# A tensor-bound backbone step: weights and moving columns placed at a fixed distance modulo 256 bytes

## The chip, the cores and the metric

The kernel runs on one core of one Trainium2 chip. The metric is the device time of one execution in microseconds (us), lower is better. The times are medians of several runs; beside them stands one execution under the hardware profiler, with its own time.

## The reference

One inference step of a two-layer backbone over 640 tokens (512 latent, 128 context) with 1024 channels. Layer 0 mixes tokens with a bidirectional state-space scan (SSD), layer 1 with differential attention. After each mixer comes a gated channel mixer with a convolution of width 3 between its two matrix products. Cut to what matters here:

```python
for i in range(DEPTH):                       # DEPTH = 2
    hp, hs = modulate(xp, ...), modulate(xs, ...)
    # mixer: i == 0: SSD; i == 1: differential attention
    op, os_ = mixer(hp), mixer(hs)
    xp = xp + p_g1 * op;  xs = xs + s_g1 * os_
    xp = xp + p_g2 * conv_ffn(modulate(xp, ...), *ffn_p)
    xs = xs + s_g2 * conv_ffn(modulate(xs, ...), *ffn_p)

def conv_ffn(h, up_w, conv_w, conv_b, down_w):
    u = dwconv(h @ up_w, conv_w, conv_b)     # 1024 -> 5632 channels
    a, v = jnp.split(u, 2, axis=-1)
    return (jax.nn.silu(a) * v) @ down_w     # 2816 -> 1024 channels
```

Everything is float32, and the products with weights are by far the most work.

## The kernel before

Activations lie channel-major: 128 channels on the partitions, the 640 tokens in a row of 2560 bytes in each partition. A float32 product is made of three fast ones: each operand is split into a high and a low part of type float32r, and the kernel adds high·high, high·low and low·high. These are called the dense products below.

A dense product is a chain of matmul instructions that add into one output. Each matmul holds a block of 128 x 128 weights in the array (the stationary operand; the profile shows its load as PEld) and streams 256, 320 or 384 columns of an activation tile past it (the moving operand). `dense_many` runs over the 8 (or 4, or 6) blocks of channels, over the three pairs high·high, high·low, low·high, and over the two halves of the tokens, "A" with 256 columns and "B" with 384, so that matmuls of 256 and 384 columns alternate and each pair of them works off 640 columns. Where one half alone is run (in `start_tiles` and at the end of `project_last`), many matmuls of one width follow each other. In the feed-forward layers, from the sixth block of channels on, `pair8` and `begin7` use a scheme with seven products instead of eight for blocks of 2 x 2 (tiles `T1` to `T3` hold sums of activations, tiles `s` sums of weights); all its matmuls have 320 columns.

While one matmul runs, the weights of the next one are loaded. So two streams read the on-chip memory at once: the moving columns of the running matmul, and the weight columns of the next one.

Tiles come from pools. `self.pw` ("wts") holds raw weights and their parts `whi` and `wlo`, three buffers each; `self.ph` ("acts") holds activations, among them the split activations with the tags `hh` and `hl` (printed as `h00h`, `h01l` and so on); in each feed-forward layer a pool of its own holds the split products `mh` and `ml`, which are the moving operand of the second matrix product, and two more buffers each for weight parts (`xhi`, `xlo`; they print as `whi` and `wlo` as well). `cast` makes the parts and chooses the pool: with a feed-forward pool open, two of every five weight units go to its `x` buffers, or a unit's own entry says so. A pool takes its address from what lies ahead of it, and a tile its address from the order in which its tag is first used. Each of these tiles, and each slice of one that a matmul takes, is a multiple of 256 bytes long in a partition, so a tag has one address modulo 256 in all of its buffers and slices.

Nearly all instructions stand under line 95 of the code, since a helper issues them; the tiles tell them apart: `po` is an output projection (from `mh`, `ml` in the feed-forward layers), `up` the first product of a feed-forward layer, `x`, `z`, `bc` the products into the scan, `q`, `k`, `v` those of the attention, `st` the first tiles after a normalization.

Of the kernel before, what the change touches and what calls it, by code (L numbers as in the profile page):

```python
# [11 lines left out]
F32 = mybir.dt.float32  # L12
# [8 lines left out]
P = 128  # L21
# [43 lines left out]
class Op:  # L65

    def __init__(self, engine, call, args, kw, dur, occ):
        self.engine, self.call, self.args, self.kw = engine, call, args, kw
        self.dur, self.occ = dur, occ
        self.real, self.end = None, 0.0  # L70
# [285 lines left out]
class Step:  # L356


    def __init__(self, ctx, tc, a):
        self.ctx, self.tc, self.nc, self.a = ctx, tc, Engines(self, tc.nc), a  # L360
        self.later = None
        self.tasks = []
        self.ticks = 0
        self.wi = 0
        self.normt = {}
        self.ready = []
        self.px = None
        self.modtask = None
        self.late = []
        self.wraw, self.wcast = {}, {}  # L370
        self.s, self.summed = {}, set()
        self.deep = 1
        self.units = []
        pool = lambda n, b, **k: ctx.enter_context(tc.tile_pool(name=n, bufs=b, **k, reuse_waits="tile"))
        self.pc = pool("const", 1)
        self.pw = pool("wts", 2)
        self.ph = pool("acts", 1)
        self.xctx = ExitStack()
        self.xd = None
        self.psb = None  # L380
        self.psm = pool("psm", 1, space=PSUM)
        self.dram = pool("dram", 1, space=bass.MemoryType.DRAM)
# [100 lines left out]
    def cast(self, upto):  # L483
        while len(self.wcast) <= min(upto, len(self.units) - 1):
            u = len(self.wcast)
            self.prefetch(u)
            n = self.units[u][1]
            r = self.wraw[u]
            kind = self.units[u][2]
            place = self.units[u][3] or ("x" if self.px and u % 5 > 2 else "w")  # L490
            wp, t, b = (self.pw, "w", 3) if place == "w" else (self.px, "x", 2)
            hi = wp.tile([P, 1024], F32R, tag=t + "hi", name=f"whi{u}", bufs=b)
            lo = wp.tile([P, 1024], F32R, tag=t + "lo", name=f"wlo{u}", bufs=b) if u else None
            if u == 0:
                half = lambda t, j: t.rearrange("p (k j m) -> p k j m", k=KT, j=2)[:, :, j, :]
                r3 = r[:, :n].rearrange("p (k m) -> p k m", k=KT)
                self.act(half(hi, 0), r3, AF.Copy)
                self.tt(half(hi, 1), r3, half(hi, 0).bitcast(F32), ALU.subtract)
            elif isinstance(kind, tuple):
                ns, j0, ia, iv = kind  # L500
                self.prefetch(u + iv)
                ra, rv = self.wraw[u + ia], self.wraw[u + iv]
                w = ns * P
                for j in range(j0, j0 + 1024 // w):
                    x = self.slot("f", f"s{j}", bufs=NF)[:, :w]
                    a, b, op = ((rv[:, :w], rv[:, w:2 * w], ALU.add), (self.s.get(0), ra[:, :w], ALU.subtract),
                                (ra[:, :w], rv[:, :w], ALU.subtract), (ra[:, w:2 * w], self.s.get(1), ALU.subtract))[j]
                    self.tt(x, a, b, op)
                    self.s[j] = x
                    c = slice(w * (j - j0), w * (j - j0 + 1))  # L510
                    self.act(hi[:, c], x, AF.Copy)
                    self.tt(lo[:, c], x, hi[:, c].bitcast(F32), ALU.subtract)
            else:
                c = slice(kind or 0, n)
                if u in self.summed:
                    with self.urgent(1.2):
                        self.act(hi[:, c], r[:, c], AF.Copy)
                        self.act(lo[:, c], r[:, c], AF.Copy, scale=-1.0)
                        self.nc.gpsimd.dma_start(lo[:, c], self.units[u][0][:, c], accum_op=ALU.add)
                else:  # L520
                    self.act(hi[:, c], r[:, c], AF.Copy)
                    self.tt(lo[:, c], r[:, c], hi[:, c].bitcast(F32), ALU.subtract)
            self.wcast[u] = (hi, lo)

    def nextw(self):
        u = self.wi
        self.wi += 1
        self.prefetch(u + 2 + self.deep)
        self.cast(u + self.deep)
        return self.wcast[u]  # L530
# [499 lines left out]
    def ffn(self, l, h, nextnorm, pool):  # L1030
# [17 lines left out]
        def epilogue(p, ua, uv):  # L1048
            ca = self.tmp("ca")
            self.conv(ca, ua, cw[:, p, :])  # L1050
            cv = self.tmp("cv")
            self.conv(cv, uv, cw[:, FT + p, :])
            self.act(ca, ca, AF.Silu)
            self.tt(cv, ca, cv, ALU.mult)
            hi = self.slot("mh", f"mh{p}", F32R, bufs=MIDS, pool=pool)
            lo = self.slot("ml", f"ml{p}", F32R, bufs=MIDS, pool=pool)
            self.act(hi, cv, AF.Copy)
            if p + 1 not in ends:
                self.act(lo, cv, AF.Copy, scale=-1.0)
                nc.gpsimd.dma_start(lo, cv, accum_op=ALU.add)  # L1060
            else:
                self.tt(lo, cv, hi.bitcast(F32), ALU.subtract)
            mid[p] = (hi, lo)
# [66 lines left out]
        def pair8(p, more):  # L1130
# [27 lines left out]
            with self.tc.high_priority():  # L1158
                self.act(uv[:, lft], X, AF.Copy)
            epilogue(p, ua, uv)  # L1160

        def finish_operands():
# [744 lines left out]
    def run(self):  # L1907
        tc, nc, a = self.tc, self.nc, self.a
        self.units = self.weight_units()
        name = lambda u: self.units[u][0] is not None and self.units[u][0].name  # L1910
        up = [u for u in range(len(self.units)) if name(u) == a["w_up"].name]
        after = {u for u in up if name(u - 1) and name(u - 1) != a["w_up"].name}
        after |= {u + 3 for u in after if name(u + 1) is False}
        half = len(up) // 2
        self.summed = (set(up) - set(up[:5]) - set(up[half:half + 5]) - after)
        qkv = [u for u in range(len(self.units)) if name(u) == a["w_qkv"].name]
        self.summed |= set(qkv[8:])
        self.x = []

        def norm(l, s, h):  # L1920
            def mk(hf):
                if hf == "A":
                    h.extend(self.new_h(f"h{l}{s}"))
                return self.norm_task(hf, self.gs[l][s], self.shift(l, s), h)
            return mk

        hs = [[] for _ in range(4)]
        psd = lambda: tc.tile_pool(name="psd", bufs=3, space=PSUM, reuse_waits="tile")
        psb = lambda: tc.tile_pool(name="psb", bufs=6, space=PSUM, reuse_waits="tile")
        self.open_x()  # L1930
        scond = ExitStack()
        sp = scond.enter_context(tc.tile_pool(name="scond", bufs=1, reuse_waits="tile"))
        with psd() as self.psd:
            with tc.tile_pool(name="first", bufs=1, reuse_waits="tile") as pool, tc.manual_schedule():
                self.silu_cond(sp)
                dtps = self.first_tiles(hs[0], pool)
            with (tc.tile_pool(name="sconst", bufs=1, reuse_waits="tile") as cp,
                  tc.tile_pool(name="ssd", bufs=1, reuse_waits="tile") as pool):
                self.ssd_consts(cp)
                self.ssd(hs[0], dtps, norm(0, 1, hs[1]), pool)  # L1940
        scond.close()
        with psb() as self.psb, tc.tile_pool(name="ffn0", bufs=1, reuse_waits="tile") as pool:
            self.px = pool
            self.late = [lambda: self.slot("f", "ntl", bufs=NF)] * 3
            self.ffn(0, hs[1], norm(1, 0, hs[2]), pool)
            self.px = None
        self.psb = None
        self.deep = 1
        with psd() as self.psd:
            self.attention(hs[2], norm(1, 1, hs[3]))  # L1950
        with psb() as self.psb, tc.tile_pool(name="ffn1", bufs=1, reuse_waits="tile") as pool:
            self.px = pool
            self.ffn(1, hs[3], self.final_task, pool)
            for t in reversed(list(self.tasks)):
                self.drain(t)
        self.xctx.close()
# [99 lines left out]
```

## Time and profile before

| | us |
|---|---|
| median of 3 runs (1797.16 to 1798.43) | 1798.12 |
| the profiled execution's own time | 1797.76 |
| its span, first to last instruction | 1796.0 |
| mean granted clock of TensorE | 0.996 |

The span falls into these stretches: up to 40 us the start; to 421 us the scan; to 548 us its output projection; to 1000 us the first feed-forward layer; to 1256 us the attention; to 1340 us its output projection; to 1796 us the second feed-forward layer. A matmul's duration in the profile is modelled and holds its passage through the array: matmuls that follow each other overlap in it. So their speed is not read from the mean duration but from the distance between their starts, here called the step.

### The profile page before, as it was taken

To read this page: it belongs to the slowest core of one execution; us is meant where nothing else is said; L and a number is where in the kernel's file an instruction comes from. 1 tells how busy PE (TensorE), PEld (TensorE's weight loads), DVE (VectorE), ACT (ScalarE), POOL (GpSimd) and SP (SyncE) were. 2 spreads that over 40 slices of the span, in tenths; PEclk is the share of its full clock that TensorE was granted. 3 is DMA by queue.
4 is the path that set the end of the run, shared out by engine and by line. 5 is a ranking of instruction groups with operands and counts; after the bars stand their busy time and mean duration, and the time that the engine had idled before them with its cause. 6 is when DMAs were issued, how large, how long until landed. Compare 5 with 4: busy or idle time off the path is not lost.

```text
span 1796.0 us, 33598 instructions
## 1 busy us (share of the span) xinstructions
PE 1763.9 (98%) x12786; PEld 1687.8 (94%) x12786; DVE 1473.8 (82%) x2947; ACT 1172.3 (65%) x2313; POOL 150.2 (8%) x180
## 2 busy tenths in 40 slices
PE   7999999999999999999999999999999999999997
PEld 5899899989989999999999999999889999999997
DVE  5789999999966869788689799899778577867686
ACT  3479696979524767667675588777547565756661
POOL 0000000000000111212210000000001112121210
PEclk9999999999999999999999999999999999999998
DMA  9844344445663686978877365665147458686882
GB/s 346 256 145 133 108 119 148 114 136 173 211 217 133 144 208 151 244 182 208 193 164 248 114 166 129 156 161 156 55 134 188 117 146 197 173 192 152 169 233 76
DMA packets 120206, 300.66 MB, mean 167 GB/s; under 512 B 13950, under 2 KB 21738, under 8 KB 120044
## 3 DMA queue, kind: packets, MB, share of 16 engines
q1 hardware_dynamic: 94636, 231.79, 39.8%
q0 software_dynamic: 24832, 66.20, 20.9%
q8 instruction: 100, 1.64, 0.4%
q14 instruction: 62, 0.51, 0.1%
q10 hardware_dynamic: 576, 0.52, 0.1%
HBM read 248.32 MB, written 34.80 MB: 158 GB/s over the span
## 4 chain that ended last, share of the span: by engine, by line
PE 71%; DVE 5%; DMA 2%; ACT 1%; issue 1%; DVEq 0%; ACTq 0%; SPq 0%
PE up L95 28%; PE po L95 24%; PE st L95 3%; PE z L95 2%; PE q L348 2%; PE v L348 2%; PE sl L348 2%; PE k L348 2%; PE ov L348 1%; PE po L348 1%; PE yp L95 1%; PE wt L348 1%; DVE sm L348 1%; PE nbc L95 1%; DMA rbc<-rsd 0%
## 5 line engine op out<-in xcount | busy, mean ns | idle before, releaser
L95 ACT ACTIVATE whi<-raw 128x1024 fp32r<-128x1024 f32 (+2 forms) x233 | 199.0, 856 | 180.2 <-PE po L95 87.3
L95 DVE TENSOR_TENSOR wlo<-raw,whi 128x1024 fp32r<-128x1024 f32 (+2 forms) x170 | 162.9, 965 | 59.4 <-ACT whi L95 58.9
L95 PE MATMUL po<-mh,whi 128*128 128x256 f32 (+1 forms) x704 | 166.3, 310 | 0.4 <-ACT y L95 0.2
L95 PE MATMUL po<-ml,whi 128*128 128x256 f32 (+1 forms) x704 | 165.9, 309 | 0.1
L95 PE MATMUL po<-mh,wlo 128*128 128x256 f32 (+1 forms) x704 | 165.7, 309 | 0.0
L95 DVE TENSOR_TENSOR wlo<-s,whi 128x512 fp32r<-128x512 f32 x136 | 91.4, 687 | 53.7 <-ACT whi L95 52.9
L95 POOL DMA_DIRECT2D wlo<-in_w_up x62 | 54.0, 871 | 953.9 <-ACT wlo L95 648.9
L95 PEld LDWEIGHTS po<-mh,whi 128*128 128x128 f32 x704 | 127.6, 188 | 1.3 <-ACT mh L95 0.6
L95 PEld LDWEIGHTS po<-ml,whi 128*128 128x128 f32 x704 | 127.8, 188 | 0.4 <-DMA ml<-cv 0.4
L95 PEld LDWEIGHTS po<-mh,wlo 128*128 128x128 f32 x704 | 128.0, 188 | 0.0
L95 PE MATMUL up<-Th,whi 128*128 128x320 f32 x408 | 126.5, 310 | 0.2 <-ACT uraw L95 0.2
L95 PE MATMUL up<-Th,wlo 128*128 128x320 f32 x408 | 126.4, 310 | 0.0
L95 PE MATMUL up<-Tl,whi 128*128 128x320 f32 x408 | 126.3, 310 | 0.0
L95 PE MATMUL up<-h11h,wlo 128*128 128x320 f32 (+2 forms) x384 | 109.5, 309 | 0.0
L95 PE MATMUL up<-h01l,whi 128*128 128x320 f32 (+2 forms) x384 | 109.5, 309 | 0.0
L95 ACT ACTIVATE whi<-s 128x512 fp32r<-128x512 f32 x136 | 83.2, 628 | 40.4 <-DVE s L95 34.4
L95 PE MATMUL up<-h01h,wlo 128*128 128x320 f32 (+2 forms) x384 | 109.5, 309 | 0.0
L95 PE MATMUL up<-h01h,whi 128*128 128x320 f32 (+2 forms) x384 | 109.5, 309 | 0.0
L95 PE MATMUL up<-h11l,whi 128*128 128x320 f32 (+2 forms) x384 | 109.5, 309 | 0.0
L95 PE MATMUL up<-h11h,whi 128*128 128x320 f32 (+2 forms) x384 | 109.5, 309 | 0.0
L95 DVE SCALAR_TENSOR_TENSOR ca<-uraw,fcw,ca 128x511 f32<-128x511 f32 (+1 forms) x176 | 86.3, 547 | 10.9 <-ACT ca L95 9.3
L95 DVE SCALAR_TENSOR_TENSOR cv<-uraw,fcw,cv 128x511 f32<-128x511 f32 (+1 forms) x176 | 85.8, 546 | 5.3 <-ACT cv L95 5.1
(574 smaller groups left out, 5438.9 us busy)
## 6 DMA issues: line engine op xcount, KB each, us to landing
raw<-in_w_up SPq DMA_DIRECT2D x88, 512.0 KB
mw<-in_modT SPq DMA_DIRECT2D x44, 512.0 KB
raw<-in_w_in SPq DMA_DIRECT2D x40, 512.0 KB
rb<-rowd SPq DMA_DIRECT2D x40, 512.0 KB
wlo<-in_w_up POOLq DMA_DIRECT2D x36, 512.0 KB, 5.6
raw<-in_w_dn SPq DMA_DIRECT2D x64, 256.0 KB
raw<-in_w_qkv SPq DMA_DIRECT2D x24, 512.0 KB
mr<-in_mod SPq DMA_DIRECT2D x44, 256.0 KB
```

What stands on the lines that cost most here:

```text
L95: return later.record(self.name, method, call, args, kw) if later else call(*args, **kw)
L348: op.real = op.call(*(x.get() if isinstance(x, Lazy) else x for x in op.args), **op.kw)
```

## The change

Three unused tiles are put into the pools. One of 128 bytes in each partition stands at the head of the pool of the activations and moves all of that pool and what lies behind it. In each feed-forward pool one stands ahead of the `x` buffers of the weights (192 bytes in the first layer, 128 in the second) and one ahead of `mh` and `ml` (128 and 64 bytes).

```diff
+        self.net = ""
...
         self.pw = pool("wts", 2)
         self.ph = pool("acts", 1)
+        self.ph.tile([P, 32], F32, tag="pad", name="pad", bufs=1)
+        self.pads = dict(ffn0=dict(x=48, m=32), ffn1=dict(x=32, m=16))
...
             wp, t, b = (self.pw, "w", 3) if place == "w" else (self.px, "x", 2)
+            if place == "x":
+                self.indent(wp, "x")
...
+    def indent(self, pool, key):
+
+        n = self.pads.get(self.net, {}).pop(key, 0)
+        if n:
+            pool.tile([P, n], F32, tag="pad" + key, name="pad" + key, bufs=1)
...
             self.tt(cv, ca, cv, ALU.mult)
+            self.indent(pool, "m")
             hi = self.slot("mh", f"mh{p}", F32R, bufs=MIDS, pool=pool)
...
             self.px = pool
+            self.net = "ffn0"
...
             self.px = pool
+            self.net = "ffn1"
```

No instruction reads or writes the new tiles. On each of the five queues the same instructions stand in the same order, with the same waits, before and after; what differs is the address of tiles. Modulo 256 bytes these addresses are (from the built programs):

| tile | before | after |
|---|---|---|
| `whi`, `wlo` in the pool `wts` | 192 | 192 |
| `whi`, `wlo` in a feed-forward pool (`x`) | 128 | 192 |
| split activations `hh`, `hl` | 192 | 64 |
| `mh`, `ml` | 128 | 64 |
| `Th`, `Tl` (sums of activations) | 224 | 224 |

The distance below is the address of the next matmul's weights less that of the running matmul's columns, modulo 256. Counted over the program (the matmuls whose distance comes to 128):

| columns | distance before | distance after | matmuls |
|---|---|---|---|
| 256 | 0 | 128 | 2858 |
| 384 | 0 | 128 | 2691 |
| 256 | 192 | 128 | 167 |
| 384 | 192 | 128 | 169 |
| 256 | 64 | 128 | 617 |
| 384 | 64 | 128 | 612 |
| 320 | 0 | 128 | 855 |
| 320 | 192 | 128 | 777 |

The 1190 matmuls with `Th` or `Tl` ahead of weights from `wts` stay at 224, and those of the attention's scores and weighted values keep their distances but for a few at the seams.

## The prediction

> **What bounds the kernel now.** I read the page's span, its busy line, the granted clock and the chain first, then the waits of TensorE.
>
> ```profile
> span 1796.0 us, 33598 instructions
> ...
> PE 1763.9 (98%) x12786; PEld 1687.8 (94%) x12786; DVE 1473.8 (82%) x2947; ACT 1172.3 (65%) x2313; POOL 150.2 (8%) x180
> ...
> PEclk9999999999999999999999999999999999999998
> ...
> PE 71%; DVE 5%; DMA 2%; ACT 1%; issue 1%; DVEq 0%; ACTq 0%; SPq 0%
> ```
>
> ```profile
> PE ms L95 <- ACT sq L95: 7.8, 3, 6.0
> PE nbc L95 <- DVE rs_y L95: 3.1, 3, 2.5
> PE st L95 <- ACT whi L95: 1.9, 1, 1.9
> ```
>
> TensorE is busy for 98% of the span, its clock is granted nearly in full, and its longest waits come to 7.8, 3.1 and 1.9 us in all. So the time is the sum of the matmuls' steps, and nothing that leaves the steps alone can move it by much. The change alters no instruction and no wait. It can act in one way only: through the addresses from which two streams read at once, the running matmul's columns and the next one's weights. The question is whether the step depends on their distance, and what it is at 128 bytes, the distance that the change gives to 8746 dense matmuls.
>
> **What the step is at the distances that the trace has.** The output projection in the first feed-forward layer is the best place to look: same instructions, no waits, and weights from two pools. The view is the timeline of TensorE; a row's first number is the start, and each row is a pair of 256 and 384 columns. The first two rows are the first and last of 24 pairs at distance 64 (the weights one 64-byte line above), the next two of 24 pairs at distance 0, the last two of 36 pairs at 64 again.
>
> ```profile
> 710.08 0.46 PE L95 MATMUL po<-mh,whi 128*128 128x256 f32 x2
> ...
> 716.98 0.46 PE L95 MATMUL po<-mh,wlo 128*128 128x256 f32 x2
> 717.27 0.46 PE L95 MATMUL po<-mh,whi 128*128 128x256 f32 x2
> ...
> 724.02 0.46 PE L95 MATMUL po<-mh,wlo 128*128 128x256 f32 x2
> 724.32 0.45 PE L95 MATMUL po<-mh,whi 128*128 128x256 f32 x2
> ...
> 734.35 0.45 PE L95 MATMUL po<-mh,wlo 128*128 128x256 f32 x2
> ```
>
> The steps of a pair are 6.90/23 = 0.300 us, 6.75/23 = 0.2935 us and 10.03/35 = 0.2866 us, or 0.4688, 0.4586 and 0.4478 ns a column: **long, neutral, short**. The same pair of instructions at the same distance, 64, runs with the long and with the short step. It is long when the stretch is entered from the 320-column matmuls, and short when it is entered from weights at distance 0. So distance 64 has two rhythms in which the streams can lock, and what came before picks one. Distance 0 has one.
>
> Now matmuls of 256 columns alone, at the start of the feed-forward layer: first 13 at distance 0, then 12 at 192, with the same moving tiles.
>
> ```profile
> 560.30 0.28 PE L95 MATMUL st<-h01l,whi 128*128 128x256 f32 x1
> ...
> 561.73 0.28 PE L95 MATMUL st<-h01l,whi 128*128 128x256 f32 x1
> ...
> 563.92 0.28 PE L95 MATMUL st<-h01h,wlo 128*128 128x256 f32 x1
> ...
> 565.17 0.28 PE L95 MATMUL st<-h01l,whi 128*128 128x256 f32 x1
> ```
>
> 1.43/12 = 0.119 us at distance 0 and 1.25/11 = 0.1136 us at 192: 5% less through the address alone. [...]
>
> Last the 320 columns: 23 matmuls at 192, 13 at distance 0, 24 of the untouched `T` tiles at 224.
>
> ```profile
> 681.90 0.31 PE L95 MATMUL up<-h01h,whi 128*128 128x320 f32 x1
> ...
> 685.12 0.31 PE L95 MATMUL up<-h01l,whi 128*128 128x320 f32 x1
> 685.27 0.31 PE L95 MATMUL up<-h01h,wlo 128*128 128x320 f32 x1
> ...
> 687.03 0.31 PE L95 MATMUL up<-h01h,wlo 128*128 128x320 f32 x1
> 687.17 0.32 PE L95 MATMUL up<-Th,whi 128*128 128x320 f32 x1
> ...
> 690.55 0.31 PE L95 MATMUL up<-Th,wlo 128*128 128x320 f32 x1
> ```
>
> 3.22/22 = 0.1464, 1.76/12 = 0.1467 and 3.38/23 = 0.1470 us: all neutral, 0.458 to 0.459 ns a column. Three distances that give one speed speak for a cost that mostly does not care.
>
> **The change part by part.** The padding tiles cost no instruction and no transfer: nothing writes them. The moves of the raw tiles, the small float32 products and the transposes change what they share with each other in address, and no row shows a price; they are some 475 us of TensorE that keep their length either way, and I take nothing. VectorE and ScalarE read and write the moved tiles too, but with 82% and 65% busy they are not the bound, and a per cent more there is hidden under TensorE.
>
> What is left are the dense matmuls. By the counts in the table of the change: at distance 0 and 192, 3025 of 256 and 2860 of 384 columns, 1,872,640 columns together; 1632 of 320, 522,240 columns; at distance 64, 392,960 columns, of which 432 matmuls (16 weight tiles, counted by the starts in the timeline, 138,240 columns) run in the long rhythm.
>
> No row shows distance 128. Its price is bounded by the nearest rows: the long pair, 0.4688 ns a column, and the lone 256s, 0.1136/256 = 0.4438. Between them lie the neutral and the short pair. I take the **short** value, 0.4478. The reasons: in both tests in which a distance other than 0 differs from 0 steadily, it is the better one (64 after the seam, 192 for lone 256s); 128 is as far from 0 as one can be; and the long rhythm is left in the trace for good as soon as a tile at another distance breaks it. The choice is close.
>
> - Pairs at 0 and 192: 1,872,640 x (0.4586 - 0.4478) = 20.2 us.
> - The 320s, at the same relative gain: 522,240 x 0.0108 = 5.6 us. No row shows a 320 stretch off neutral, so the other bound is 0.
> - The tiles at 64 in the long rhythm: 138,240 x (0.4688 - 0.4478) = 2.9 us. Those in the short one gain nothing.
>
> Together 28.7 us. Not all of it reaches the end, since VectorE is near its own limit in two stretches (the windows: length, then TensorE, weight loads and VectorE busy):
>
> ```profile
> 40.00:421.00 381.00, 379.40 (x2953) 347.14 (x2946) 348.92 (x699) 287.92 (x663) 0.00 (x0) 1.00 0.47 147
> ...
> 632.00:965.00 333.00, 332.48 (x2263) 331.34 (x2262) 265.71 (x481) 223.53 (x412) 62.01 (x72) 1.00 0.80 198
> ...
> 1000.00:1256.00 256.00, 254.54 (x1755) 242.07 (x1755) 234.81 (x511) 195.33 (x395) 13.74 (x16) 1.00 0.59 151
> ```
>
> In the scan and the attention VectorE is busy for 92% (348.92 of 381, 234.81 of 256), in the feed-forward layer for 80%. The dense matmuls of the scan hold 575,616 columns and those of the attention 337,280, so 912,896 x 0.0108 = 9.9 us of the gain arise there. I let half of it, 4.9 us, be lost in waits for VectorE: those chains are late next. That leaves 23.8 us. From the profiled execution's 1797.8 us the sum is **1774 us**; that execution lies 0.4 us under the median of the runs, which I leave out.
>
> [...]
>
> **The rivals.**
>
> *The distance does not matter on average.* For it: 0, 192 and 224 give the same step in the 320s, and 0 and 192 nearly so elsewhere; the short and the long rhythm at 64 lie evenly around it. If the weight stream sweeps past the column stream, each load costs the same wherever it starts. Then the neutral 0.4586 holds everywhere. The tiles at 64 go neutral as well: 138,240 x 0.0102 = 1.4 us saved, 254,720 x 0.0108 = 2.8 us lost, and the lone 256s at distance 0, some 270 in the timeline, save 270 x 0.006 = 1.6 us. **1798 us.** Against it: the two rhythms, and 0.119 against 0.1136. [...]
>
> *The long rhythm locks in.* The place is the seam from 320-column matmuls into pairs, where distance 64 always began in the long rhythm in the quoted layer. In the changed kernel no tile at another distance follows in the projection, so nothing breaks the rhythm. It decides from the point at which 128 locks like 64 after such a seam, and the stretches without 320s follow. The price is 1,872,640 x 0.0102 + 522,240 x 0.0102 + 254,720 x 0.021 = 29.8 us: **1827 us**; with only the feed-forward projections and some pairs caught, about 1805 to 1815. For it: the tiles with the long step are there, at a distance one line away. Against it: no stretch outside 64 shows it.
>
> *All of it at the lowest step in the trace.* At 0.4438 ns a column the gains are 2,394,880 x 0.0148 + 138,240 x 0.025 + 254,720 x 0.004 = 39.9 us, **1758 us** with nothing lost to VectorE.
>
> **How the numbers follow.** The short rhythm and its variants, the lowest step among them, hold 0.49; no effect 0.26; the long rhythm in whole or part 0.25. The forecast is 1774 us, the likeliest; its own range is 1750 to 1790. A measurement of this kernel can tell about 0.2%, 3.6 us, from no change. Faster by more than that: 0.49; within: 0.26; slower: 0.25. For 8 in 10 the range takes in the short rhythm down to 1748, no effect, and the long rhythm in a part of the stretches up to 1815. What is left out is the long rhythm everywhere (0.14) and a gain deeper than any row shows (0.05).
>
> **What would show it.** In the changed profile, a pair's step in the feed-forward projection: 0.287 us in all eight tiles is my case, 0.2935 the first rival, 0.300 the second. The 320s at 0.1434 instead of 0.1467 us carry the 5.6 us; at 0.1467 that term is gone. The `T` tiles must keep about 0.147: if they move, something other than the distance acts. Waits of TensorE on VectorE in the scan and the attention should grow by some 5 us; if they grow by 10, the halving was too kind. The forecast is wrong if two rhythms show again at 128, or if waits move elsewhere though no instruction did.

## The result, and the profile after

| | before | after |
|---|---|---|
| median, us | 1797.86 (4 runs) | 1787.79 (4 runs, 1785.78 to 1791.21) |
| span of the profiled execution, us | 1796.0 | 1785.8 |

The ratio is 0.9949, 95% interval [0.9936, 0.9962]; in a second batch with ten runs of the changed kernel (1785.0 to 1796.0 us) it was 0.9971 [0.9959, 0.9983]. So the change saves 0.3 to 0.5%. The forecast was 1774 us, a saving of 24 us where 10 were measured in the first batch; the sign and the range held, the size did not. In the second batch the median was 1792.93 us, above the forecast's own range of 1750 to 1790, though within the wider one up to 1815.

The page of the changed kernel: span, busy line, granted clock, chain.

```profile
span 1785.8 us, 33598 instructions
...
PE 1751.6 (98%) x12786; PEld 1675.0 (94%) x12786; DVE 1472.3 (82%) x2947; ACT 1170.8 (66%) x2313; POOL 150.4 (8%) x180
...
PEclk9999999999999999999999999999999999999998
...
PE 71%; DVE 6%; ACT 2%; DMA 1%; issue 1%; DVEq 0%; ACTq 0%
```

It reads as before: TensorE, busy for 98% of the span, bounds the kernel at a mean granted clock of 0.997 (0.996 before), and its busy time fell by 12.3 us. Its longest waits hardly moved:

```profile
PE ms L95 <- ACT sq L95: 8.1, 3, 6.4
PE nbc L95 <- DVE rs_y L95: 3.0, 3, 2.5
PE st L95 <- ACT whi L95: 1.8, 1, 1.8
```

Now the steps, in the timeline of TensorE, at distance 128 throughout. Ahead of each group stands how many rows it has; the first and the last are shown. First 84 pairs of the output projection in the first feed-forward layer, where the kernel before had all three rhythms:

```profile
706.41 0.45 PE L95 MATMUL po<-mh,whi 128*128 128x256 f32 x2
...
730.21 0.45 PE L95 MATMUL po<-mh,wlo 128*128 128x256 f32 x2
```

23.80/83 = 0.2867 us: the short rhythm, as forecast. Then 168 pairs at the start of the same layer:

```profile
577.94 0.46 PE L95 MATMUL up<-h01h,whi 128*128 128x256 f32 x2
...
628.04 0.46 PE L95 MATMUL up<-h01h,wlo 128*128 128x256 f32 x2
```

50.10/167 = 0.300 us: long, where the kernel before had the neutral step of distance 0. Last 14 lone 256s, 36 of the 320s, and 24 of the untouched `T` tiles:

```profile
554.44 0.28 PE L95 MATMUL st<-h01l,whi 128*128 128x256 f32 x1
...
555.98 0.28 PE L95 MATMUL st<-h01h,wlo 128*128 128x256 f32 x1
...
678.25 0.31 PE L95 MATMUL up<-h01h,whi 128*128 128x320 f32 x1
...
683.38 0.31 PE L95 MATMUL up<-h01h,wlo 128*128 128x320 f32 x1
683.53 0.31 PE L95 MATMUL up<-Th,whi 128*128 128x320 f32 x1
...
686.91 0.31 PE L95 MATMUL up<-Th,wlo 128*128 128x320 f32 x1
```

1.54/13 = 0.1185 us (0.119 at distance 0), 5.13/35 = 0.1466 and 3.38/23 = 0.1470 us. The 320s gained nothing. So there are two rhythms at 128 too. Counted over the trace (short is a step under about 290 ns, long one over about 297, neutral between): 2218 pairs short, 541 long, 216 neutral; before 370, 339 and 2269.

### The profile page after: what moved, and what is told of

Same layout as the page of the kernel before. It is cut to its first block, busy times and chain, and to the rows that moved or that the text cites. A ratio compares the mean times of both kernels' runs of the same rounds, so it can differ in the third digit from the quotient of the medians.

```text
span 1785.8 us, 33598 instructions
## 1 busy us (share of the span) xinstructions
PE 1751.6 (98%) x12786; PEld 1675.0 (94%) x12786; DVE 1472.3 (82%) x2947; ACT 1170.8 (66%) x2313; POOL 150.4 (8%) x180
## 3 DMA queue, kind: packets, MB, share of 16 engines
q1 hardware_dynamic: 94636, 231.79, 40.4%
## 4 chain that ended last, share of the span: by engine, by line
PE 71%; DVE 6%; ACT 2%; DMA 1%; issue 1%; DVEq 0%; ACTq 0%
PE up L95 28%; PE po L95 24%; PE st L95 3%; PE v L348 2%; PE q L348 2%; PE k L348 2%; PE sl L348 2%; PE ov L348 1%; PE po L348 1%; PE z L95 1%; PE wt L348 1%; PE yp L95 1%; PE nbc L95 1%; DVE wlo L95 0%; PE modrow L95 0%
```

## The experiments

Steps below are distances between the starts of matmuls in the trace, in ns; a pair has 640 columns.

**1. The step at 16 distances.** A kernel of its own: for each distance pairs after a pause, then lone 256s, 320s and 384s with pairs behind each.

```diff
+DISTANCES = tuple(range(0, 256, 16))
...
+                        nc.tensor.matmul(tile_(n)[:, :n], w[:, b + 128 * wi + e:b + 128 * wi + e + 128],
+                                         x[:, T * xi + c0:T * xi + c0 + n], start=k <= len(seq),
```

> Not the backbone: only chains of the dense matmuls on two loaded tiles, at 16 distances (0, 16, ... 240 bytes) of the next weights from the running columns; the outputs are zeros. At each distance, after a pause: pairs of 256 and 384 columns, lone 256s, pairs, 320s, pairs, lone 384s, pairs. Theory A (the distance modulo 256 picks a rhythm): pairs step 0.2935 us at 0 and 192, and 0.287 or 0.300 us at 64 and 128, the entry picking which; the 320s 0.1467 us everywhere. Rival B (the distance is nothing, the layout of the large kernel acts in another way): pairs step the same, within 0.5%, at all 16 distances. Rival C (a step that grows with nearness to 0): the shortest pairs at 128, rising evenly to both sides.

| distance | pair after a pause; behind 256s; 320s; 384s | 256 | 320 | 384 |
|---|---|---|---|---|
| 0 | 293 in all four | 120.0 | 146.6 | 173.4 |
| 48 | 286.7 in all four | 122.7 | 144.3 | 173.4 |
| 64 | 286.6; 286.6; 300.0; 300.0 | 113.4 | 146.6 | 176.6 |
| 112 | 300.1; 293.4; 299.9; 293.2 | 119.5 | 146.6 | 173.4 |
| 128 | 286.7; 286.6; 286.6; 300.0 | 118.5 | 146.8 | 176.5 |
| 144 | 300.0 in all four | 119.9 | 146.6 | 177.4 |
| 192 | 293.4 in all four | 117.7 | 146.8 | 173.4 |

The other nine lie between 289 and 297 in pairs. The step does depend on the distance (pairs of 286.6 to 300.1 ns), and distance 128 has two rhythms (286.6 and 300.0 ns). Nearness to 0 does not order the list: 48 is the best (286.7 ns in all four places) and 144 the worst (300.0).

**2 to 4. All dense operands at 64, at 0, at 192.** Only the sizes of the padding tiles differ from the changed kernel.

```diff
-        self.ph.tile([P, 32], F32, tag="pad", name="pad", bufs=1)
-        self.pads = dict(ffn0=dict(x=48, m=32), ffn1=dict(x=32, m=16))
+        self.ph.tile([P, 48], F32, tag="pad", name="pad", bufs=1)
+        self.pads = dict(ffn0=dict(x=32, m=48), ffn1=dict(x=16, m=16))
```

> All dense operands at distance 64 instead of 128. Theory A: two rhythms as at 128, pairs 0.287 or 0.300 us, time 1784 to 1794 us. Rival C: 64 is half as far from 0 as 128, so about half of the gain, 1792 us, with one step for all pairs. Rival B: 1797 to 1799 us or any other time.

> All dense operands at distance 0, with tiles moved as much as in the change. Theory A and rival C: pairs 0.2935 us, time 1797 to 1800 us. Rival B (moving tiles is what helps): a gain as in the change, 1786 to 1790 us.

> All dense operands at distance 192. Theory A: pairs 0.2935 us, lone 256s 0.1136 us, time 1795 to 1799 us. Rival C: as far from 0 as 64, so the time of the run at 64.

| distance | ratio to before | pairs short / long / neutral |
|---|---|---|
| 64 | 0.9976 [0.9966, 0.9986] | 1492 / 1267 / 222 |
| 0 | 1.0001 [0.9992, 1.0011] | 22 / 79 / 2877 |
| 192 | 1.0002 [0.9992, 1.0012] | 32 / 47 / 2896 |

Moving the tiles as such is worth nothing here, as far as these runs go. They do not match the change byte for byte: run 4 (192) moves the activations by 64 bytes where the change moves them by 128, and run 3 (0), other than its expectation says, leaves the activations in place and moves only tiles in the feed-forward pools, by 64 bytes. Run 2 (64) moves the activations further than the change, by 192 bytes, and gains no more. Of these three only 64, with 1492 short pairs, gains. At 64, where more than four in ten pairs are long, the gain is half of that of the first batch of the changed kernel; against its second batch, 0.9971, the intervals overlap.

**5. Finer distances, and another order.** The chains again, 24 to 68 bytes in steps of 4, then 128, 0, 64, 48, with the 384s first.

> As e1_steps, with distances 24 to 68 by 4, then 128, 0, 64 and 48, and the order pairs, lone 384s, pairs, lone 256s, pairs, 320s, pairs. Theory A (distance picks the rhythm, at some distances two are stable and the entry picks): 48 again 0.2867 us for all pairs and 0.144 us for the 320s; 128 and 64 long (0.300) after lone 384s; whether 256s and 320s bring 128 back to short is open. Rival D (what e1_steps showed at 48 was chance of one order): 48 shows another step here.

The windows of this run (length of the window, then busy times); each spans 10 whole pairs of a steady stretch, the third 9: 48; 52; 128 after the pause; 128 behind 384s; 128 behind 256s; 0; 64 behind 384s; 64 behind 320s.

```profile
262.04:264.91 2.87, 2.87 (x21) 2.87 (x21) 0.00 (x0) 0.00 (x0) 0.00 (x0) 1.00 0.00 0
300.78:303.71 2.93, 2.93 (x21) 2.93 (x21) 0.00 (x0) 0.00 (x0) 0.00 (x0) 1.00 0.00 0
485.12:487.70 2.58, 2.58 (x20) 2.58 (x19) 0.00 (x0) 0.00 (x0) 0.00 (x0) 1.00 0.00 0
496.08:499.08 3.00, 3.00 (x21) 3.00 (x21) 0.00 (x0) 0.00 (x0) 0.00 (x0) 1.00 0.02 5
505.98:508.85 2.87, 2.87 (x22) 2.87 (x22) 0.00 (x0) 0.00 (x0) 0.00 (x0) 1.00 0.00 0
534.88:537.82 2.94, 2.94 (x22) 2.94 (x21) 0.00 (x0) 0.00 (x0) 0.00 (x0) 1.00 0.02 6
573.72:576.58 2.86, 2.86 (x21) 2.86 (x21) 0.00 (x0) 0.00 (x0) 0.00 (x0) 1.00 0.00 0
593.87:596.87 3.00, 3.00 (x21) 3.00 (x21) 0.00 (x0) 0.00 (x0) 0.00 (x0) 1.00 0.00 0
```

2.87/10 = 0.287 at 48 and 2.93/10 = 0.293 at 52: four bytes make 6 ns a pair. At 128 the pairs went from 0.287 to 0.300 behind lone 384s and back to 0.287 behind lone 256s. It looked as if the kind of the matmuls ahead chose the rhythm. Runs 9, 10 and 12 test that.

**6 to 8. Distance 48**, which had one rhythm in the chains, the short one (286.7 ns). Weights in the middle of longer tiles give it. By their sizes these take 10 x 256 = 2560 bytes more in a partition, as much as one activation buffer, and all three runs do without one of those: run 6 is the changed kernel with that buffer gone, 7 adds the distance, 8 brings the `T` tiles to 48 as well.

```diff
-NF = 11
+NF = 10
...
-            hi = wp.tile([P, 1024], F32R, tag=t + "hi", name=f"whi{u}", bufs=b)
+            hi = wp.tile([P, 1088], F32R, tag=t + "hi", name=f"whi{u}", bufs=b)[:, 4:1028]
...
+            tp.tile([P, 16], F32, tag="padt", name="padt", bufs=1)
```

> The change with 10 instead of 11 buffers of one activation tag, which frees room for the next two runs; a control. If that buffer is not on the path: 1785 to 1791 us as with the change.

> All dense operands at distance 48 (the weight parts lie 16 bytes into slightly longer tiles), 10 buffers as in e6_nf10. Theory A: pairs 0.2867 us everywhere with no long ones, 320s 0.144 us, lone 256s 0.1227 us; against e6_nf10 541 long pairs x 13.3 ns = 7.2 us and 1632 x 2.4 ns = 3.9 us less, 1.5 us more for lone 256s: 1776 to 1781 us. Rival C (nearness to 0 is bad): slower than at 64, over 1793 us.

> As e7_d48, and the sums of activations in the 320-column scheme at distance 48 too. Theory A: another 1190 x 2.5 ns = 3 us less than e7_d48, 1773 to 1778 us.

Run 6: 1.0056 [1.004, 1.0071], 1804.83 us, a miss: against the ratios of the changed kernel, 0.9971 and 0.9949, the buffer is worth 15 to 19 us (a wait of `po` on VectorE of 7.5 us is new in its trace). Run 7: 0.9994 [0.9984, 1.0003], 1795.39 us, 9.4 us less than run 6; the 1776 to 1781 us that were expected missed by what the buffer costs. Its pairs are 2326 short, 602 neutral and 29 long (the chains at 48 showed no neutral ones; why the kernel does stays open), and 36 of its 320s, in the timeline, show the gain that the prediction wanted of them, 5.05/35 = 0.1443 us:

```profile
675.97 0.31 PE L95 MATMUL up<-h01h,whi 128*128 128x320 f32 x1
...
681.02 0.31 PE L95 MATMUL up<-h01h,wlo 128*128 128x320 f32 x1
```

From mean pairs of 290.04 to 287.89 ns, 2957 of them, 6.4 us; 1632 320s x 2.2 ns, 3.6 us: 10.0 us. Between the two traces the lone matmuls took 1.1 us of it back, and 9.4 were measured. Run 8: 0.9985 [0.9976, 0.9995], 1.6 us less again where 3 were expected; the two intervals overlap, but in the traces the steps of the `T` tiles fell from 146.4 to 144.9 ns, 1.9 us in all. The distance works (9.4 us), the memory it takes does not pay (15 to 19 us).

**9 to 11. The order of the matmuls ahead.** The first up tile of each feed-forward layer and the first tile of each output slice run as two chains of lone matmuls; all else is the changed kernel. Run 9 ends them in 256s ("BA"), run 10 in 384s ("AB"); run 11 is the changed kernel again, in the same batch.

```diff
+    def apart(self, ps, w, ks, h):
+
+        for p in "BA":
+            self.dense_many([(ps, w, P)], ks, h, p, hook=p == "A")
...
-            self.dense(ps, self.nextw(), ks, h)
+            (self.apart if self.net and i == 0 else self.dense)(ps, self.nextw(), ks, h)
```

> The changed kernel with the same matmuls in another order in two kinds of place: in the first up-projection tile of each feed-forward layer, and in the first output tile of each output-projection slice, all lone 384-column matmuls come first and then all lone 256-column ones, where there were pairs of both; every later tile runs in pairs as before. Nothing is added or left out. Theory (at distance 128 lone 384s bring the long rhythm and lone 256s the short one, and pairs keep what they find): every projection of both feed-forward layers is entered in the short rhythm, 0.2866 us a pair. The 264 long pairs from the start of the first layer to its first output slice go short: 264 x 13.3 ns = 3.5 us less than the changed kernel of the same batch, about 1784 us, and no stretch of long pairs in the feed-forward layers. Rival (the rhythm is chance, or set by the pauses at a stage's start, and the kind of matmul ahead has no say): the same time as the changed kernel within 1 us, and long stretches somewhere in the feed-forward layers.

> The same edit with the order the other way about: lone 256s first, then lone 384s, then the tiles in pairs. The same matmuls at the same addresses as in the run that ends in 256s. Theory: every projection of the feed-forward layers is entered in the long rhythm, 0.300 us a pair. Of some 1160 pairs about 900 are short in the changed kernel: 900 x 13.3 ns = 12 us more than the changed kernel, about 1800 us, and 15 us more than the run that ends in 256s. Rival: within 1 us of that run.

> The changed kernel once more, in the same batch as the two orders. Theory: 1786 to 1791 us; of the stretches in the profile, the one from 578 to 657 us is long again, since lone 384s end the stage ahead of it, and the short stretches of the scan and the attention fall where they fall: a few hundred pairs more or fewer in the long rhythm, 13.3 ns each, are the 2 to 5 us by which its runs differ. Rival (the rhythm is fixed by the program): the same counts, 541 long and 2218 short pairs, to within ten.

Run 9: 1800.37 us, 1.0024 [1.0014, 1.0034]. Run 10: 1796.82, 0.9998 [0.9986, 1.001]. Run 11: 1792.93, where 1786 to 1791 were expected. The theory fell: the order that should have been short is the longer one. Here are pairs in the same slice of the projection, from the timelines: first run 9 (61 rows), then run 10 (64 rows):

```profile
713.94 0.46 PE L95 MATMUL po<-mh,wlo 128*128 128x256 f32 x2
...
731.94 0.28 PE L95 MATMUL po<-mh,wlo 128*128 128x256 f32 x1
```

```profile
713.80 0.45 PE L95 MATMUL po<-mh,whi 128*128 128x256 f32 x2
...
731.86 0.45 PE L95 MATMUL po<-mh,whi 128*128 128x256 f32 x2
```

18.00/60 = 0.300 behind 256s, 18.06/63 = 0.2867 behind 384s. The up tile of run 9, with 24 lone 256s instead of 12, was left in the short rhythm. And run 11 differs from the first profile of the same program: here the end of the attention's projection, 11 rows each, first profile, then run 11:

```profile
1307.00 0.45 PE L95 MATMUL po<-o6l,whi 128*128 128x256 f32 x2
...
1309.86 0.45 PE L95 MATMUL po<-o7h,wlo 128*128 128x256 f32 x2
```

```profile
1308.35 0.46 PE L95 MATMUL po<-o6l,whi 128*128 128x256 f32 x2
...
1311.35 0.46 PE L95 MATMUL po<-o7h,wlo 128*128 128x256 f32 x2
```

2.86/10 against 3.00/10. From there to 1440 us run 11 has 275 long pairs; in all it has 848, 307 more than the first profile.

What tells the entries (the places where a stretch of pairs begins) apart are the steps just ahead. Lone 384s at 128 run in a pattern of five, lone 256s in another (from the starts in the trace; the last 256 ahead of "then" is the first pair's own):

```
run 9,  up, short:   256: 115 118 121 120 120 115   then 384:173 256:120 384:168
run 9,  po, long:    256: 115 118 121 120 119       then 384:173 256:122 384:175
run 10, po, short:   384: 175 181 176 174 174       then 256:116 384:175 256:120 384:168
changed kernel, up, long: 384: 176 173 174 175 182  then 256:119 384:181 256:119 384:181
```

New theory: the place in that pattern at which the lone matmuls stop sets the rhythm, and pairs keep it until another width or a wait comes.

**12. Counts instead of kinds.** Chains at 128 and 64: 20 to 24 lone matmuls after a pause, then 24 pairs.

> Only chains of matmuls on two tiles, and the outputs are filled with zeros: everything else is left out. For distance 128 and then 64: 15 stretches, each after a pause; a stretch is a run of lone matmuls of 384, 320 or 256 columns, 20, 21, 22, 23 or 24 of them, and 24 pairs straight behind. In the changed kernel and in the two orders, lone 384s at 128 run in a pattern of five steps (about 174, 174, 175, 182, 176 ns), and lone 256s in one of five (115, 118, 122, 120, 119). Theory (the rhythm of the pairs is set by the place in that pattern at which the lone matmuls stop, not by their kind): at 128 the pairs behind lone 384s are long (0.300 us) where the last or the last but one step was the one of 182 ns, short (0.2866 us) where three shorter steps followed it; so among the five counts some are long and some short, and the same holds behind 256s. Rival (kind decides, as the earlier chains had it): all five counts of 384s give long pairs, all five of 256s short ones. Second rival (chance): no order in the counts.

In the trace three lone 256s stand between the lone matmuls and the pairs in all stretches but the first. Windows of 14 pairs (the first row) or 11, at 128: behind 20 to 24 lone 384s, then behind 20 to 24 lone 256s.

```profile
18.52:22.73 4.21, 4.21 (x30) 4.21 (x30) 0.00 (x0) 0.00 (x0) 0.00 (x0) 1.00 0.91 352
30.48:33.63 3.15, 3.15 (x24) 3.15 (x23) 0.00 (x0) 0.00 (x0) 0.00 (x0) 1.00 0.00 0
41.58:44.73 3.15, 3.15 (x23) 3.15 (x23) 0.00 (x0) 0.00 (x0) 0.00 (x0) 1.00 0.00 0
52.96:56.26 3.30, 3.30 (x24) 3.30 (x23) 0.00 (x0) 0.00 (x0) 0.00 (x0) 1.00 0.00 0
64.69:67.99 3.30, 3.30 (x23) 3.30 (x23) 0.00 (x0) 0.00 (x0) 0.00 (x0) 1.00 0.03 5
127.48:130.78 3.30, 3.30 (x24) 3.30 (x23) 0.00 (x0) 0.00 (x0) 0.00 (x0) 1.00 0.00 0
137.39:140.54 3.15, 3.15 (x23) 3.15 (x23) 0.00 (x0) 0.00 (x0) 0.00 (x0) 1.00 0.00 0
147.25:150.40 3.15, 3.15 (x23) 3.15 (x23) 0.00 (x0) 0.00 (x0) 0.00 (x0) 1.00 0.00 0
157.31:160.61 3.30, 3.30 (x23) 3.30 (x23) 0.00 (x0) 0.00 (x0) 0.00 (x0) 1.00 0.00 0
167.67:170.97 3.30, 3.30 (x23) 3.30 (x23) 0.00 (x0) 0.00 (x0) 0.00 (x0) 1.00 0.00 0
```

Both kinds give both rhythms (4.21/14 and 3.30/11 = 0.300 us, 3.15/11 = 0.286), long, short, short, long, long in either. With the three 256s in between, only the first stretch goes from lone 384s straight into pairs, so this run alone would not clear the kind; with the slices of runs 9 and 10, where 256s led to long and 384s to short pairs, the kind is out. The count matters. Over all 15 stretches at 128 there are 7 short and 8 long, at 64 there are 9 and 6.

**13 to 18. The count in the kernel.** At the start of the first feed-forward layer the last matmuls of the third tile (1 to 5 of each width) are held back and run as pairs, so that the lone 384s stop elsewhere; nothing is added.

```diff
+                        if keep and ps is tiles[-1][0]:
+                            self.kept.append(one)
+                        else:
+                            self.mm(*one)
...
+        for ab in zip(*held):
+            for one in ab:
+                self.mm(*one)
```

> The changed kernel with one edit of order: at the start of the first feed-forward layer the last two matmuls of the third tile, in their 256-column and their 384-column part, are held back and run as two pairs at the end of the stage. So 70 lone 384s precede the first pair instead of 72; the same work, nothing added. Theory (the place in the five-step pattern at which the lone 384s stop sets the rhythm): 72 end on the step of 182 ns and the pairs are long; 70 end three shorter steps after it, if the pattern starts as before, and the 264 pairs up to 657 us run short: 264 x 13.3 ns = 3.5 us less than with five held back. If two 256s fewer start the pattern elsewhere, the last steps say so: short behind three shorter steps, long behind the 182 or the one after it. Rival (what precedes has no say in the place, only in the kind): long, as in the changed kernel.

> The same edit with five matmuls held back instead of two: 31 lone 256s and 67 lone 384s, five fewer of each, then five pairs, and the projection. Theory: five is one whole pattern, so the lone 384s stop on the step of 182 ns as in the changed kernel, and the 264 pairs up to 657 us are long, 0.300 us each; 3.5 us more than with two held back, where that one runs short. Rival (any pairs that are put ahead of the projection, or fewer lone 384s, bring the short rhythm): short as well, the same time as with two.

> One matmul of the third tile's two parts held back: 71 lone 384s and one pair ahead of the projection. What the runs so far say, in steps after the one of 181 to 183 ns in the five-step pattern of lone 384s: stopped on it, long; one step behind it, long; three behind it, short; four behind it, long; two is open. Theory: this map holds here too, whatever number the pattern starts from. The start moves with the number of lone 256s ahead, so the place is read from the last steps: a stop three behind gives 0.2866 us a pair up to 657 us, a stop at nought, one or four behind 0.300 us. Rival (the place has no say): a long stretch behind three, or a short one behind nought, one or four.

> Three held back: 69 lone 384s and three pairs ahead of the projection. The same map: nought, one and four steps behind the one of 182 ns long, three behind it short, two open. The rival as in the run with one held back.

> Four held back: 68 lone 384s and four pairs ahead of the projection. The same map: nought, one and four steps behind the one of 182 ns long, three behind it short, two open. The rival as in the run with one held back. If one of the three runs is short up to 657 us, it should lie 3.5 us under the one that is long, as far as the other stretches agree.

> The order with four held back once more, timed in five rounds as the best candidate: it is the one whose lone 384s stop two steps behind the one of 182 ns, and the first layer's pairs ran short from the start. Theory: the stretch up to 657 us is short again, since the pauses ahead of it end alike; the entries behind a wait in the scan, in the attention and at the second feed-forward layer fall anew. With 264 pairs turned, the median lies 3.5 us under what the changed kernel gave on average in its two batches (a ratio of 0.9949 and 0.9971 to the kernel before), so a ratio of about 0.994. Rival (the gain is lost at other entries, which fall long as often as short): a ratio of 0.996 to 0.997, as for the changed kernel.

| held back | lone 384s stop, in steps behind the long one | pairs from there to 657 us | time, us |
|---|---|---|---|
| 0 (changed kernel, both profiles) | 0 | long | 1787.79; 1792.93 |
| 1 | 0 | long | 1795.37 (one run) |
| 2 | 0 | long | 1789.84 |
| 3 | another pattern (174, 175, 177) | short | 1788.33 (one run) |
| 4, first profile | 2 | short | 1788.61 (one run) |
| 4, profile of the timed batch | 4 | long | 1788.74 |
| 5 | 4 | long | 1792.5 |

The timelines with 1 and with 4 held back (first profile), 101 and 105 rows of the same tiles:

```profile
589.81 0.46 PE L96 MATMUL up<-h01h,whi 128*128 128x256 f32 x2
...
619.81 0.46 PE L96 MATMUL up<-h01l,whi 128*128 128x256 f32 x2
```

```profile
589.91 0.45 PE L96 MATMUL up<-h01h,wlo 128*128 128x256 f32 x2
...
619.72 0.45 PE L96 MATMUL up<-h01l,whi 128*128 128x256 f32 x2
```

30.00/100 = 0.300, 29.81/104 = 0.2866. The forecast from the count alone missed with 2 (long, not short); with 5 the pairs were long as forecast, but the lone 384s stopped at another place than the count gave. The pattern did not start where I took it to start. Read from the last steps, the rule held. Over the ten profiles at 128 that have the stage, 25 entries come from lone 384s in the pattern of five: on the long step 9, all long; one behind it 4, all long; two behind 1, short; three behind 9, all short; four behind 2, both long. Of 68 entries from 320s, the 66 from a pattern of 145 and 148 are short, the 2 from one of 146 and 147 long. The stop two steps behind has one case only, and the place fell as it did by itself: no run set it.

No order was found that beats the changed kernel for good. With 4 held back the timed ratio is 0.996 [0.9948, 0.9972] where 0.994 was expected, no better than the changed kernel: the same program fell short once and long once at the same place.

## Why the prediction was wrong in its size

**What bounds the kernel; nothing else moves.** Right as far as it was tried. Distances 0 and 192, with part of the tiles moved, gave 1.0001 and 1.0002.

**The step that failed: the short value for all pairs.** The prediction put 0.4478 ns a column on every pair at 128, with two tests in favour, and left the long rhythm to a rival. In the trace of after 2218 of 2975 pairs have it. Two rhythms at 128 were the sign of being wrong that the prediction itself had named. Matching the matmuls of both traces one to one, those in pairs that do not wait went from 904.5 to 893.7 us: 10.8 us less, where the two terms for pairs had 20.2 + 2.9 = 23.1. The rest has two parts. 541 long pairs x 13.3 ns and 216 neutral ones x 6.7 are 8.6 us. And both terms took all columns of 256 and 384 as pairs: 461 x 256 + 581 x 384 of them are not in such pairs, 341,000 x 0.0108 = 3.7 us. Most are in lone matmuls (some 455 of each width in the trace), which at 128 gain nothing (118.8 ns against 120 and 113, 176.0 against 173.4). 10.8 + 8.6 + 3.7 = 23.1. With the 320s, the `T` tiles among them (0.5 less), the lone matmuls (0.7 more), the other products (2.0 less) and all waits (2.0 more) the matching comes to 10.6 us; the spans differ by 10.2.

**Why that could not come out as forecast.** At 128 the rhythm went not by the distance but by each entry (of the 25 from lone 384s 15 were long, 10 short), and long and short lie evenly around the neutral step (300.0 and 286.6 ns around 293.4 in the chains). The first rival said that of 64 and drew the mean; it was beaten only because more entries fell short. Spans against long pairs, for the changed kernel and the orders that hold back; the last row leaves out the start, up to the matmul that stands at 40.1 us in the kernel before:

| long pairs | 541 | 550 | 655 | 769 | 848 | 939 | 944 | 982 |
|---|---|---|---|---|---|---|---|---|
| span, us | 1785.8 | 1786.6 | 1786.8 | 1788.6 | 1790.6 | 1793.6 | 1790.8 | 1792.7 |
| without the start | 1748.0 | 1746.4 | 1747.6 | 1749.2 | 1751.3 | 1754.2 | 1752.8 | 1755.2 |

From 541 to 982, 441 pairs, are 441 x 13.3 ns = 5.9 us; 6.9 were measured, 7.2 without the start. An estimate from these: with half of the 2975 long, 947 more than in the first profile, the span would be 1785.8 + 12.6 = 1798.4 us, no better than before. So the saving, and most of the spread between these profiles, is how the entries fell. It is not all chance: in all eight, 18 to 33% of the pairs are long and never half, and part of that repeats, since 66 of the 68 entries from 320s were short, while of the 25 from the pattern of lone 384s 15 were long. Neither had been forecast.

**The 320s.** The other bound was right: 0.1466 us, and the 1632 of them took 239.3 us before and 239.5 after, where 5.6 were to be saved. The 0.5 us above are those of the `T` tiles, whose distance did not change; runs 3 and 4 show them too (0.6 and 0.5). A distance that lowers the 320s exists (48: 0.1443).

**Half of the scan's gain lost to VectorE.** Right in the scan, too hard in the attention. Between the same instructions in the two traces (40 to 421 us before), free pairs (those that do not wait) gained 3.8 us and matmuls that wait lost 1.8, most of it to VectorE; in the attention (1000 to 1300 us) pairs gained 1.1 and waits took 0.1.

**A term that was not in the sum.** The first 40 us became 2.6 us shorter, 2.2 of it in float32 products that were costed at nothing. The windows of before, of after and of run 11, the changed kernel again, show a granted clock (third number from the end) of 0.96, 1.00 and 0.96 there:

```profile
0.00:40.00 40.00, 29.66 (x339) 20.25 (x343) 22.57 (x45) 14.83 (x24) 0.20 (x4) 0.96 0.99 354
```

```profile
0.00:40.00 40.00, 28.86 (x373) 20.06 (x374) 24.63 (x49) 15.70 (x25) 0.20 (x4) 1.00 0.97 346
```

```profile
0.00:40.00 40.00, 29.22 (x363) 20.29 (x363) 23.25 (x46) 15.61 (x25) 0.20 (x4) 0.96 0.98 351
```

One and the same matmul starts at 40.1, 37.8 and 39.3 us in the three. The order with four held back had 0.96 in its first profile and 1.00 in its second (39.2 and 38.0 us). Over all 17 profiles of the backbone it starts at 37.5 to 38.0 us in the four with 1.00 and at 38.8 to 40.4 us in the 13 with 0.96. So the clock at the start differs between executions of one program, and of the 10.2 us between the first two profiles some 1.5 us (37.8 against 39.3 for the same program) was luck and not the change.

**The rivals.** The long rhythm did come, in 18 and 28% of the pairs in the two profiles, but not at the seam named: at 128, 66 of the 68 entries from 320s were short, and those after lone matmuls and pauses go either way. That the seam brought it at 64 was right (run 5, and half of the pairs of run 2). All of it at the lowest step was excluded by the lone 256s (118.5 ns at 128, where 113.6 were taken). No run shows the streams themselves: that they lock or sweep past each other, and that 64 bytes are a line, are the author's pictures. The runs show steps alone, at distance 64 pairs of 286.6 and 300.0 ns.

## What to carry to other kernels

Where TensorE is busy all the time (98% here), look at the distance between the addresses of the next weights and the running columns, modulo 256: in the chains one and the same pair of matmuls took 286.6 to 300.1 ns by that and what ran ahead alone, and the lone 256s 113.4 to 123.4. Prefer a distance at which chains show one short rhythm whatever ran ahead (here 48, 286.7 ns) to one that has two (64, 128: 286.6 and 300.0), and weigh the memory that it takes: here one buffer cost more (15 to 19 us) than the distance gave (9.4). A step seen in one stretch is not the step of its distance until the same distance has been seen to be entered in several ways.

## What the runs showed of the hardware

- **Many steady steps come near whole multiples of 6.67 ns.** In run 1 a lone matmul at distance 0 takes 120.0 ns with 256 columns and 173.4 with 384: 53.4/128 = 0.417 ns a column, 6.67 ns for 16 columns. The measured 113.4, 120.0, 146.6, 173.4, 286.6, 293.4 and 300.0 ns lie within 0.3 ns of 17, 18, 22, 26, 43, 44 and 45 of these; at 0.417 ns a column, an estimate from that difference, the columns alone would make 16, 16, 20, 24, 40, 40 and 40. The two rhythms at 128 (300.0 and 286.6 ns) differ by two of them in a pair, and each lies one from the neutral step (293.4). Not every step fits: pairs of 296.6 and 291.5 ns (distances 80 and 56) and 320s of 144.3 ns (48) do not. What the rest above the columns is spent on was not shown.
- **Four bytes count.** In run 5 pairs at 44, 48, 52 took 293.3, 286.7, 293.4 ns; lone 256s 117.5, 123.4, 113.4. So of these the best distance for pairs is the worst for lone 256s.
- **What ran ahead counts, and for long.** At 128 a pair's step (286.6 or 300.0 ns) went with the place at which the matmuls ahead stopped in their pattern, in all 25 entries from the pattern of lone 384s, and it lasted for 264 pairs on end (from 577.94 to 657.14 us in the profile after, 0.300 us each). What in the chip keeps it was not shown.
- **The same program differs between executions** by 11 us (1785.0 to 1796.0 in run 11). The profiles show two parts of it: 13.3 ns for each pair that turns from short to long (307 pairs, 4.1 us, between the two profiles of the changed kernel) and the granted clock of the first 40 us (1.00 and 0.96; one matmul starts at 37.8 and 39.3 us there).
